# Layer 0's modulation chunks 4 to 11 by ScalarE products and GpSimd sums

## The chip, the cores and the metric

The kernel runs on one core of one Trainium2 chip. The metric is the device time of one execution in microseconds, the median of three runs: 1533.48 before the change (1533.36 to 1533.84). A profile of one execution shows where the time lies. Its engines are PE (TensorE's matmuls), PEld (its weight loads, which overlap PE), DVE (VectorE), ACT (ScalarE), POOL (GpSimd) and SP (SyncE, whose queue starts the loads of weights). Every engine works through its own queue in order.

## The reference

A trunk of two layers works on 512 latent and 256 context tokens of 1024 features. The part that the change touches is the modulation: one vector product for each of two conditions, 6144 columns per layer, which are cut into twelve chunks of 512.

```python
def modulation(cond, w_mod, b_mod):
    m = jax.nn.silu(cond) @ w_mod + b_mod
    return m.reshape(m.shape[:-1] + (N_MOD, D_MODEL))
...
        m_lat = modulation(c, w_mod[l], b_mod[l])
        m_ctx = modulation(c_ctx, w_mod[l], b_mod[l])
        sh1, sc1, ga1, sh2, sc2, ga2 = [m_lat[:, i, None, :] for i in range(N_MOD)]
        csh1, csc1, cga1, csh2, csc2, cga2 = [m_ctx[None, i, None, :] for i in range(N_MOD)]
...
        x_lat = x_lat + ga1 * (jnp.concatenate([attn_lat, gm_lat], axis=-1) @ w_out[l])
        x_lat = x_lat + ga2 * sqrelu_mlp(modulate(rmsnorm(x_lat, norm2_g[l]), sh2, sc2),
                                         w_ff1[l], w_ff2[l])
```

Chunks 0 to 3 are the shift and scale of the first norm. Chunks 4 and 5 are the gate ga1, wanted when the output projection begins. Chunks 6 to 9 are the shift and scale of the second norm, and 10 and 11 the gate ga2 of the MLP. Between norm and gate stand the input projection, a gated mixer (gMLP), grouped-query attention with eight query heads, and one output projection over both. In the last layer the context tokens get no gate and no MLP, so that there only the first four chunks are used for the context condition.

## The kernel before

Activations lie feature by feature, 128 features on the partitions and up to 768 tokens along a row. Every float32 product is made of three passes over numbers split into a high and a low part: `split` casts the high part on ACT (L207) and subtracts it for the low part on DVE or POOL (L208).

The stages of layer 0 follow one another on PE: the first chunks of the modulation and the projection of keys and values, the projections u and g of the mixer, the queries in six banks of 256 tokens, then attention, then the output projection (`proj4`), the second norm, and the MLP with ff1 and ff2. Layer 1 does the same again.

The order of the work around the change is set by `Flow`, an emission clock that counts PE time: `defer` puts work off by so many ns of that clock. Attention is written tile by tile: 16 tiles of context queries (256 keys), then 32 of latent queries (768 keys). A tile is a product of queries and keys (L203, `pa<-B,B`), its maximum on DVE (L825), the exponential on ACT (L828), the reciprocal on DVE (L830), which POOL spreads (`rc`, L833), later transposes on PE (L844) that ACT and DVE split (L846, L847), and then the product with the values (`pb<-A,B`), which closes with a matmul that reads `rc` (L865). After each tile a filler step is emitted on PE. The string `FILL0` orders these fillers: pieces of the output projection of the mixer (`o`, twelve matmuls of 128x384) and pieces of chunks 4 to 11 (`m`).

A piece of `mod_chunk` is one weight block of 128x1024, that is 32x512 matmuls in the four 32-column strips of PE (L326). After four pieces DVE turns the four partial sums (L334), four small matmuls add them (L339), and `mod_store` adds the bias (L391). Its weight blocks use the four slots of the ring `hi`, which the split weights use too.

Layer 1's modulation is made differently: `mod_wide` runs beside the MLP of layer 0. For each half weight block of 128x512 and each condition ACT makes a product with a scalar per partition (L365, L368) into a tile `s`, and POOL adds it to an accumulator (L369). After eight of them DVE turns and sums each condition (L380, L381). The accumulator is one tile in the place `C1`, the raw weights are two halves of a tile `k`. The tiles `s` have three buffers for the whole kernel; the activations of the projections, the mixer and the norms use the same three.

Of the kernel before, what the change touches and what calls it, by code (L numbers as in the profile page):

```python
# [8 lines left out]
F32 = mybir.dt.float32  # L9
# [7 lines left out]
KT = 8  # L17
# [9 lines left out]
# columns of the packed constants  # L27
# [4 lines left out]
# emission lags and periods, in ns of tensor-engine time  # L32
# [9 lines left out]
def once(fn):  # L42
    """fn, but for the first call alone"""
    left = [fn]
    return lambda: left.pop()() if left else None


class Flow:
    """Emission clock: counts tensor-engine time and emits put-off work once its turn has come."""

    def __init__(self):
        self.vt = 0.0
        self.todo = []
        self.n = 0
        self.fillers = []
        self.busy = False

# [5 lines left out]
    def tick(self, ns=0.0):  # L63
# [22 lines left out]
    def fill0(self, until):  # L86
        """pass the time without fillers"""
# [4 lines left out]
    def step(self):  # L92
        """one piece of filler"""
# [9 lines left out]
    def drain(self):  # L103
        """Emit everything put off, with fillers in between."""
# [8 lines left out]
# how pieces of the output projection (o) and of the modulation (m) alternate beside the attention of layer 0  # L113
FILL0 = "oooooooommmommmmmmmmmommmmommmommmomoomo"
# [5 lines left out]
def block_order():  # L120
    o = []
    mod = lambda j: [("mod", 0, j, kb) for kb in range(4)]
    tok = lambda l, g: [("tok", l, g, kb) for kb in range(2)]
    for l in range(DEPTH):
# [10 lines left out]
        if l == 0:  # L135
            o += mod(4) + mod(5)
            rest = mod(6) + mod(7) + mod(8) + mod(9) + mod(10) + mod(11)
            n = 0
            for c in FILL0:
                if c == "m":  # L140
                    o.append(rest.pop(0))
                else:
                    if n % 4 == 0:
                        o.append(("out", 0, 0, n // 4))
                    n += 1
            o += rest
        else:
            o += [("out", l, 0, nb) for nb in range(4)]
        o += [("out", l, 1, nb) for nb in range(4)]
# [11 lines left out]
def trunk(ctx: ExitStack, tc: tile.TileContext, xT, pk1, pk2, rope, wsT, w_mod, w_tok, w_u, w_out, w_ff1, w_ff2, outT):  # L161
# [57 lines left out]
    def convert():  # L219
        """split the oldest block that is held back"""  # L220
# [53 lines left out]
    def rsqrt(v, n):  # L274
        """1/sqrt of a small positive tile: a bit estimate, a quadratic and a cubic step."""
# [26 lines left out]
    # silu of both conditions  # L302
# [12 lines left out]
    def mod_chunk(l, j, lag=1200.0):  # L315
        """512 columns of the modulation of both conditions, four partial sums at a time in the four
        32-column strips of the tensor engine; yields between weight blocks."""
        ps = pb()
        ns = PAR["NS"] if j < 4 else 4
        rows = ns * 32  # L320
        for kb in range(4):
# [6 lines left out]
            if l or j > 3:  # L328
                release()
            if kb < 3:  # L330
                yield
        # 32 by 32 blocks turned, then the strips added
        tr = (tw if l == 0 and j < 4 else tsm)([128, 512])
# [13 lines left out]
    def mod_wide(l):  # L347
        """The modulation of one layer on the vector engine; yields after each half of a weight block."""
        raw = tk([128, 2, 512], F32)

        def load(i):
            j, k = divmod(i, KT)
            if j < 12:
                (nc.gpsimd if PAR["MQ"] else nc.sync).dma_start(raw[:, k % 2, :], w_mod[l, j, k // 2][:, (k % 2) * 512:(k % 2) * 512 + 512])
        load(0)
        for j in range(12):
            acc = unit("C1", [128, 2, 512], F32)
            for k in range(KT):
                w = raw[:, k % 2, :]
# [803 lines left out]
```

## Time and profile before

| | us |
|---|---|
| median of three runs | 1533.48 |
| span of the profiled execution | 1530.9 |
| PE busy in it | 1484.1 |
| DVE busy | 957.4 |
| ACT busy | 682.6 |
| POOL busy | 402.0 |

The span is the time from the first to the last instruction of the profiled execution; 2.6 us lie around it in the median. The matmul rows of PE are pipelined, so that the mean of one is longer than what it adds to the chain. In the chain of work that ended last each step is followed back to what released it. A row of the stretches gives, between two times from the span's start, how long each engine was busy, with the number of instructions in brackets.

### The profile page before, as it was taken

The numbers are of one execution on the slowest core, as the hardware profiler recorded it, in microseconds if no ns is written. First come the engines' busy times: TensorE is split into PE (matmuls) and PEld (weight loads), VectorE is DVE, ScalarE is ACT, GpSimd is POOL, SyncE is SP. The second block draws the span as 40 slices with busy tenths as digits, with TensorE's granted clock in tenths as the row PEclk, the third lists the DMA queues.
The fourth block names the chain that finished last, engine by engine and source line by source line (L and its number), as shares of the span: only waits on it lengthen the run. The fifth ranks groups of instructions, "written<-read, shape, count | busy, mean of one in ns | idle before, by whom it ended". The sixth has DMA issues, their size and how long they took to land.

```text
span 1530.9 us, 22786 instructions
## 1 busy us (share of the span) xinstructions
PE 1484.1 (97%) x8804; PEld 1321.5 (86%) x8804; DVE 957.4 (63%) x1874; ACT 682.6 (45%) x1142; POOL 402.0 (26%) x362
## 2 busy tenths in 40 slices
PE   6999899999999999999999999998999999999998
PEld 2899686779899999999999998996889888888887
DVE  5868966776855555555555547988796644444443
ACT  3542355564545453545444424535784433322221
POOL 0112320023244545545454603035213000000000
PEclk9999999999999999999999999999999999999999
DMA  9221324321134333333333321221101333332332
GB/s 359 67 74 48 119 91 152 110 83 56 62 108 122 113 123 126 111 118 106 124 109 124 98 68 56 86 80 44 41 1 56 97 96 97 98 97 97 96 98 79
DMA packets 49948, 148.83 MB, mean 97 GB/s; under 512 B 5424, under 2 KB 6832, under 8 KB 49840
## 3 DMA queue, kind: packets, MB, share of 16 engines
q1 hardware_dynamic: 49264, 146.46, 29.9%
q8 instruction: 69, 1.13, 0.3%
q10 hardware_dynamic: 576, 0.92, 0.2%
q14 instruction: 39, 0.32, 0.1%
HBM read 145.26 MB, written 2.10 MB: 96 GB/s over the span
## 4 chain that ended last, share of the span: by engine, by line
PE 82%; DVE 12%; DMA 2%; ACT 2%; issue 1%; POOL 0%; SPq 0%; ACTq 0%; POOLq 0%; DVEq 0%
PE pa L203 51%; PE pb L203 21%; PE pt L844 3%; PE pt L203 3%; PE pb L326 2%; DVE lo L208 1%; DMA X<-in_xT 1%; DMA C<-in_w_mod 1%; DVE X L784 1%; DMA A<-in_w_mod 1%; DVE m L277 1%; PE pt L626 1%; DVE B L961 1%; ACT hi L207 1%; PE pb L865 0%
## 5 line engine op out<-in xcount | busy, mean ns | idle before, releaser
L203 PE MATMUL pa<-A,hi 128*128 128x384 f32 (+2 forms) x1696 | 449.2, 347 | 1.7 <-ACT w L954 0.6
L207 ACT CAST hi<-raw 128x1024 fp32r<-128x1024 f32 x171 | 179.5, 1050 | 409.9 <-PE pa L203 326.3
L208 DVE TENSOR_TENSOR lo<-raw,hi 128x1024 fp32r<-128x1024 f32 x155 | 202.7, 1308 | 215.8 <-ACT hi L207 212.4
L203 PEld LDWEIGHTS pa<-A,hi 128*128 128x128 f32 x1696 | 304.7, 188 | 25.9 <-ACT w L954 1.8
L369 POOL TENSOR_TENSOR C<-C,s 128x512 f32<-128x512 f32 x168 | 240.5, 1463 | 245.0 <-ACT s L368 244.8
L203 PE MATMUL pa<-A,lo 128*128 128x384 f32 (+2 forms) x848 | 293.4, 347 | 1.1 <-DVE lo L208 1.1
L203 PE MATMUL pa<-B,hi 128*128 128x384 f32 (+1 forms) x900 | 246.4, 356 | 4.4 <-DVE X L784 4.4
L203 PEld LDWEIGHTS pa<-B,hi 128*128 128x128 f32 x900 | 162.9, 188 | 21.5 <-DVE X L784 9.2
L784 DVE SCALAR_TENSOR_TENSOR X<-pa,modT,X 128x384 f32<-128x384 f32 (+1 forms) x168 | 88.0, 547 | 143.0 <-PE pa L203 143.0
L203 PEld LDWEIGHTS pa<-A,lo 128*128 128x128 f32 x848 | 159.3, 188 | 12.0 <-DVE lo L208 1.3
L203 PE MATMUL pa<-B,lo 128*128 128x384 f32 (+1 forms) x450 | 158.1, 353 | 0.0
L203 PE MATMUL pb<-B,hi 128*128 128x256 f32 (+2 forms) x600 | 152.3, 340 | 0.4 <-DVE X L784 0.4
L368 ACT ACTIVATE s<-k,silu 128x512 f32<-128x512 f32 x168 | 114.3, 716 | 49.4 <-DMA k<-in_w_mod 27.3
L203 PE MATMUL pb<-hi,A 128*128 128x256 f32 x672 | 126.1, 285 | 0.0
L784 DVE SCALAR_TENSOR_TENSOR X<-pb,modT,X 128x512 f32<-128x512 f32 (+3 forms) x116 | 69.1, 602 | 75.8 <-PE pb L203 75.3
L203 PEld LDWEIGHTS pb<-B,hi 128*128 128x128 f32 x600 | 104.0, 189 | 11.6 <-DVE X L784 1.0
L203 PEld LDWEIGHTS pb<-hi,A 128*128 128x128 f32 x672 | 106.1, 191 | 0.2 <-issue 0.2
L203 PE MATMUL pb<-B,lo 128*128 128x256 f32 (+2 forms) x300 | 101.5, 338 | 0.0
L203 PE MATMUL pb<-lo,A 128*128 128x256 f32 x336 | 95.3, 284 | 0.0
L203 PEld LDWEIGHTS pa<-B,lo 128*128 128x128 f32 x450 | 84.4, 188 | 5.8
L847 DVE TENSOR_TENSOR A<-pt,A 128x384 fp32r<-128x384 f32 (+1 forms) x144 | 73.6, 535 | 16.4 <-ACT A L846 14.4
L846 ACT CAST A<-pt 128x384 fp32r<-128x384 f32 (+1 forms) x144 | 64.6, 469 | 43.3 <-PE pt L844 39.5
(169 smaller groups left out, 2300.3 us busy)
## 6 DMA issues: line engine op xcount, KB each, us to landing
raw<-in_w_ff SPq DMA_DIRECT2D x128, 512.0 KB, 3.5
k<-in_w_mod SPq DMA_DIRECT2D x96, 256.0 KB, 3.0
hi<-in_w_mod SPq DMA_DIRECT2D x32, 512.0 KB, 3.6
raw<-in_w_tok SPq DMA_DIRECT2D x19, 512.0 KB, 3.5
raw<-in_w_out SPq DMA_DIRECT2D x16, 512.0 KB, 3.5
A<-in_w_mod SPq DMA_DIRECT2D x8, 512.0 KB, 9.9
raw<-in_w_u SPq DMA_DIRECT2D x8, 512.0 KB, 3.5
B<-in_w_mod SPq DMA_DIRECT2D x6, 512.0 KB, 10.2
```

Source lines behind the costliest of these rows:

```text
L203: pe.matmul(out, a, b, start=start, stop=stop)
L207: act.copy(hi, src)
L208: (eng or vec).tensor_tensor(out=lo, in0=src, in1=hi.bitcast(F32), op=ALU.subtract)
L277: vec.tensor_scalar(yi, v.bitcast(I32), -0.5, 1595932665.0, op0=ALU.mult, op1=ALU.add)
L326: pe.matmul(ps[q:q + 32, :], S32[:, k, :], w[:, k2 * 512:(k2 + 1) * 512], start=k < ns, stop=k >= KT - ns)
L368: act.activation(p, w, AF.Copy, scale=s)
L369: pool_e.tensor_tensor(out=a, in0=a, in1=p, op=ALU.add)
L626: pe.transpose(p[:, o:o + 128], stk[:, t, hh, c0:c0 + 128].bitcast(F32), ident)
L784: vec.scalar_tensor_tensor(out=xs, in0=src[:, s - off:e - off], scalar=modT[l][:, i * 8 + m, cond:cond + 1], in1=xs, op0=ALU.mult, op1=ALU ...
L844: pe.transpose(tp_[:, (kt - k0) * 128:(kt - k0) * 128 + 128], p[:, kt * 128:kt * 128 + 128], ident)
L846: act.copy(pth[:, k0:k0 + step, d], src)
L847: vec.tensor_tensor(out=ptl[:, k0:k0 + step, d], in0=src, in1=pth[:, k0:k0 + step, d].bitcast(F32), op=ALU.subtract)
```

## The change

Chunks 4 to 11 of layer 0 leave PE and are made by `mod_wide`, as layer 1's were. A generator in `Flow.tick` emits one step (half a weight block: two products, two sums) every 4600 ns of the emission clock from the start of layer 0 (`BG`). The turning and summing on DVE is put off by 7000 ns (`MD`), and the small matmuls by another 7000 (`ME`). There are now three raw tiles `mr`, loaded two steps ahead, and two accumulators `macc` in turn. The weight stream has no blocks of chunks 4 to 11 any more. In layer 1 chunks 4 to 11 are made for one condition alone. `FILL0` now says after which tiles a piece of the output projection is emitted. The scratch that dynamic DMA reserves is set to 2048 bytes. Comments and checks of order are left out below.

```diff
+        while self.bg is not None and self.bgt <= self.vt:
+            self.bgt += next(self.bg, 1e9)
...
-FILL0 = "oooooooommmommmmmmmmmommmmommmommmomoomo"
+FILL0 = "1101101101101101" + "01000100010001000100100100100100"
...
-        if l == 0:
-            o += mod(4) + mod(5)
-            rest = mod(6) + mod(7) + mod(8) + mod(9) + mod(10) + mod(11)
...
-        o += [("out", l, 1, nb) for nb in range(4)]
+        o += [("out", l, w, nb) for w in range(2) for nb in range(4)]
...
-        ns = PAR["NS"] if j < 4 else 4
+        ns = PAR["NS"]
...
-    def mod_wide(l):
-        """The modulation of one layer on the vector engine; yields after each half of a weight block."""
-        raw = tk([128, 2, 512], F32)
+    def mod_wide(l, js, period=0.0):
+
+
+        raws = [const.tile([128, 512], F32, tag=f"mr{i}", name=nm("mr")) for i in range(3)] if not mraw else mraw
+        mraw.extend(raws[len(mraw):])
+        steps = [(j, k) for j in js for k in range(KT)]
...
+        for i in range(2):
+            load(i)
+        acc = None
+        for i, (j, k) in enumerate(steps):
+            conds = range(2 if l == 0 or j < 4 else 1)
+            if k == 0:
+                acc = const.tile([128, 2, 512], F32, tag="macc%d" % (j % 2), name=nm("macc"))
+            load(i + 2)
+            w = mraw[i % 3]
+            for cond in conds:
+                a, s = acc[:, cond, :], sc[:, k, cond:cond + 1]
+                if k == 0:
+                    act.activation(a, w, AF.Copy, scale=s)
+                else:
+                    p = tsm([128, 512])
+                    act.activation(p, w, AF.Copy, scale=s)
+                    pool_e.tensor_tensor(out=a, in0=a, in1=p, op=ALU.add)
+            if k < KT - 1:
+                yield period
+                continue
+            fl.defer(PAR["MD"], lambda l=l, j=j, acc=acc, n=len(conds): mod_sums(l, j, acc, n))
+            yield period
+        yield 1e9
+
+    def mod_sums(l, j, acc, n):
+
+        part = tmp.tile([128, 32], F32, tag="mp", name=nm("mp"), bufs=2)[:, 0:16 * n].rearrange("p (c b) -> p c b", c=n)
+        for cond in range(n):
+            tr = tsm([128, 512])
+            vec.transpose(tr, acc[:, cond, :])
+            vec.tensor_reduce(out=part[:, cond, :], in_=tr.rearrange("p (b i) -> p b i", i=32), axis=AX.X, op=ALU.add)
+
+        def fin():
+            p4 = pt((128, n, 4))
...
+        fl.defer(PAR["ME"], fin)
...
-                                fl.step()
+                                if FILL0[nt[0]] == "1":
+                                    fl.step()
+                                nt[0] += 1
                                 fl.fill0(goal)
...
-                fl.fillers = [mods((4, 5)), mixed(fl.fillers[0], mods((6, 7, 8, 9, 10, 11))), fl.fillers[1]]
...
-        wide = None if last else mod_wide(l + 1)
+        wide = None if last else mod_wide(l + 1, range(12))
...
+    fl.bg, fl.bgt = mod_wide(0, range(4, 12), PAR["BG"]), fl.vt
...
-    nc = _bacc.Bacc("TRN2", target_bir_lowering=False, num_devices=1)
+    nc = _bacc.Bacc("TRN2", target_bir_lowering=False, num_devices=1, dynamic_dma_scratch_size=2048)
```

Three places show what this does to the order of the engines. The first is PE's queue where attention begins, before the change: `pa<-B,B` are the first tiles' products of queries and keys, `32x512` the pieces of chunk 4, `pt<-c,w` the transposes of the first tiles.

```order
L203 MATMUL pa_2082<-B_107_486,B_249_1611 128x256
L203 MATMUL pa_2082<-B_108_487,B_249_1611 128x256
L326 MATMUL pb_2094<-hi_1853,S_86 32x512 x2
L626 MATMUL pt_2097<-c_70,k_2035 128x128 x4
L626 MATMUL pt_2103<-c_70,k_2035 128x128 x4
L203 MATMUL pa_2116<-B_107_486,B_249_1611 128x256
L203 MATMUL pa_2116<-B_108_487,B_249_1611 128x256
L326 MATMUL pb_2094<-hi_1855,S_86 32x512 x2
L326 MATMUL pb_2094<-hi_2130,S_86 32x512 x2
L326 MATMUL pb_2094<-hi_2132,S_86 32x512 x2
L844 MATMUL pt_2111<-c_70,w_2087 128x128 x2
```

The same place now, where `128x384` is the first piece of the output projection, `A` the mixer's split output and `mp` the sums of chunk 6.

```order
L193 MATMUL pa_2305<-B_107_486,B_295_1766 128x256
L193 MATMUL pa_2305<-B_108_487,B_295_1766 128x256
L193 MATMUL pb_2329<-A_388_2317,hi_2038 128x384
L381 MATMUL pt_2343<-mp_2176,c_70 32x8 x4
L627 MATMUL pt_2349<-c_70,k_2251 128x128 x4
L193 MATMUL pa_2380<-B_107_486,B_295_1766 128x256
L193 MATMUL pb_2329<-A_388_2317,hi_2038 128x384
L193 MATMUL pb_2329<-A_388_2317,lo_2039 128x384
L193 MATMUL pb_2329<-A_389_2320,hi_2038 128x384
L193 MATMUL pa_2380<-B_108_487,B_295_1766 128x256
```

The pieces of the modulation are gone, and the output projection of the mixer stands in their place, ahead of the first transposes. Over the whole kernel PE's queue has 39 rows fewer.

The second place is POOL's queue at the first context tiles, before the change. `rc` spreads a reciprocal, `lo` is the low part of a weight block of the output projection, `k` that of a query bank.

```order
L833 COPY rc_2092<-m_2090 128x64
L833 COPY rc_2126<-m_2124 128x64
L833 COPY rc_2092<-m_2151 128x64
L833 COPY rc_2126<-m_2176 128x64
L208 TENSOR_TENSOR lo_2242<-raw_2239,hi_2241 128x1024
L833 COPY rc_2215<-m_2213 128x64
L208 TENSOR_TENSOR lo_2275<-raw_2272,hi_2274 128x1024
L833 COPY rc_2255<-m_2253 128x64
```

The same place now; `macc` is an accumulator, `s` a product from ACT.

```order
L835 COPY rc_2315<-m_2313 128x64
L615 TENSOR_TENSOR k_2407<-w_2187,k_2407 128x8x64
L362 TENSOR_TENSOR macc_2148<-macc_2148,s_2416 128x512
L835 COPY rc_2390<-m_2388 128x64
L362 TENSOR_TENSOR macc_2148<-macc_2148,s_2419 128x512
L835 COPY rc_2315<-m_2430 128x64
L362 TENSOR_TENSOR macc_2148<-macc_2148,s_2495 128x512
L835 COPY rc_2390<-m_2448 128x64
L362 TENSOR_TENSOR macc_2148<-macc_2148,s_2498 128x512
L835 COPY rc_2511<-m_2509 128x64
L362 TENSOR_TENSOR macc_2148<-macc_2148,s_2549 128x512
```

A sum of the modulation now stands between each two `rc`. POOL has 24 such sums between the first and the last `rc` of the context tiles and 28 among those of the latent tiles. Ahead of the first `rc` it has 46, and the low parts of the first four weight blocks of the output projection now stand there too, of which it had none there before. ACT's queue has 54 products ahead of the first exponential, 26 among the 16 context tiles, 34 among the 32 latent tiles and 14 from there to the start of the MLP.

The third place is DVE's queue in the fourth of the six query banks, before the change (`m` are sums and roots of a row, `G` the rotation's table).

```order
L593 TENSOR_REDUCE m_1888<-s_1886 128x8
L597 TENSOR_TENSOR w_1890<-pb_1816,G_150 128x512
L601 TENSOR_TENSOR s_1892<-pb_1816,G_150 128x8x32 x2
L606 TENSOR_SCALAR m_1888<-m_1888 128x8
L602 TENSOR_TENSOR w_1890<-w_1890,s_1892 128x512
L277 TENSOR_SCALAR m_1897<-m_1888 128x8
L280 TENSOR_TENSOR m_1899<-m_1897 128x8
L281 SCALAR_TENSOR_TENSOR m_1899<-m_1899,m_1888 128x8
```

The same bank now.

```order
L594 TENSOR_REDUCE m_2086<-s_2084 128x8
L598 TENSOR_TENSOR w_2088<-pb_1992,G_150 128x512
L602 TENSOR_TENSOR s_2090<-pb_1992,G_150 128x8x32 x2
L607 TENSOR_SCALAR m_2086<-m_2086 128x8
L375 STREAM_TRANSPOSE s_2177<-macc_1536 128x512
L603 TENSOR_TENSOR w_2088<-w_2088,s_2090 128x512
L267 TENSOR_SCALAR m_2095<-m_2086 128x8
L376 TENSOR_REDUCE mp_2176<-s_2177 128x16
L270 TENSOR_TENSOR m_2097<-m_2095 128x8
L375 STREAM_TRANSPOSE s_2180<-macc_1536 128x512
L271 SCALAR_TENSOR_TENSOR m_2097<-m_2097,m_2086 128x8
L376 TENSOR_REDUCE mp_2176<-s_2180 128x16
```

The two transposes and two sums of chunk 6 now lie inside this bank's work. Those of chunks 4 and 5 lie earlier, in the mixer's projections, and those of 7 to 11 later.

More of the change, by code (lines that the diff above doesn't have):

```diff
@@ L457, in apply @@
             l, w, off, n, cond = self.l, self.w, self.off, self.n, self.cond
+            assert all((l, w * 6 + k // 4 + i) in stored for k in ks for i in (0, 2))
             B = lambda k: modT[l][:, w * 24 + k, cond:cond + 1]
@@ L898, in gm_out @@
             yield from proj4(("out", l, 0), GM, 2, [dense], "b")
-        def mods(js):
-            for j in js:
-                yield from mod_chunk(0, j)
-        def mixed(a, b):
-            for c in FILL0:
-                next(a if c == "o" else b)
-                yield
-            yield from a
-            yield from b
         if last:
```

67 lines of the change are left out of this document (16 added, 51 removed), and 2 rows, old and new, of the table PAR.

## The prediction

> **What bounds the kernel now.** First the page's busy times and its chain, to see which engine sets the end.
>
> ```profile
> span 1530.9 us, 22786 instructions
> PE 1484.1 (97%) x8804; PEld 1321.5 (86%) x8804; DVE 957.4 (63%) x1874; ACT 682.6 (45%) x1142; POOL 402.0 (26%) x362
> PE 82%; DVE 12%; DMA 2%; ACT 2%; issue 1%; POOL 0%; SPq 0%; ACTq 0%; POOLq 0%; DVEq 0%
> ```
>
> PE is busy for 97% of the span, so work taken from PE counts unless something takes its place. Next the table of stretches, cut where the stages of layer 0 change: mixer's projections to 121 us, queries to 178, context tiles to 226, latent tiles, their tail with the output projection, second norm, start of the MLP, the MLP. The last row is a stretch of layer 1's attention.
>
> ```profile
> core 0: us, PE busy (x) PEld busy (x) DVE busy (x) ACT busy (x) POOL busy (x), PEclk, DMA share, GB/s
> 56.00:121.00 65.00, 64.34 (x463) 62.30 (x462) 50.60 (x166) 31.83 (x59) 8.87 (x8) 1.00 0.22 66
> 121.00:178.00 57.00, 56.61 (x471) 55.26 (x470) 49.22 (x158) 19.52 (x31) 16.04 (x12) 1.00 0.16 47
> 178.00:226.00 48.00, 40.60 (x258) 32.33 (x257) 32.87 (x92) 24.60 (x68) 14.07 (x22) 0.93 0.40 134
> 226.00:338.00 112.00, 110.43 (x694) 78.30 (x693) 79.07 (x168) 64.73 (x143) 16.52 (x35) 1.00 0.36 118
> 338.00:376.00 38.00, 37.97 (x259) 34.15 (x258) 22.61 (x51) 16.26 (x33) 12.02 (x13) 1.00 0.13 42
> 376.00:402.00 26.00, 25.02 (x153) 21.82 (x151) 20.36 (x42) 11.66 (x22) 7.72 (x5) 1.00 0.19 62
> 402.00:440.00 38.00, 36.97 (x181) 32.38 (x182) 27.95 (x43) 22.28 (x35) 7.81 (x5) 1.00 0.28 87
> 440.00:900.00 460.00, 456.49 (x2677) 447.80 (x2676) 247.88 (x337) 216.19 (x289) 232.64 (x164) 1.00 0.37 114
> 1100.00:1140.00 40.00, 39.84 (x295) 36.41 (x293) 37.92 (x81) 36.19 (x83) 6.92 (x22) 1.00 0.00 1
> ```
>
> PE bounds all of layer 0 but 178 to 226, where it idles 7.4 us. DVE is close behind it in the query banks (49.2 of 57). ACT and POOL have room everywhere. The last row shows that this kernel can run PE at 99.6% with DVE at 95% and ACT at 90%.
>
> **What PE loses.** The group of L326 over the layer's `hi` blocks, and two rows of the chain, one a piece of the modulation and one a piece of the output projection:
>
> ```profile
> L326 PE MATMUL pb<-hi,S 128*32 128x512 f32 x128 | 36.6, 612 | 0.9 <-DMA hi<-in_w_mod 0.9
> 288.48 0.98 PE pb L326 x4
> 236.20 2.09 PE pb L203 x12
> ```
>
> 128 matmuls are 32 pieces of four. The 36.6 us count pipelined overlap; a piece stands 0.98 us in the chain, so 32 x 0.98 = **31.4 us** leave PE. The small adding matmuls stay, four to a chunk. In the new order 8 of the pieces leave the context tiles and 24 the latent ones.
>
> **What ACT, POOL and DVE gain.** The new kind of work is the one that layer 1's modulation does during the MLP:
>
> ```profile
> 479.24 1.94 ACT L368 ACTIVATE s<-k,silu 128x512 f32<-128x512 f32 x3
> L369 POOL TENSOR_TENSOR C<-C,s x164: 1272/1294/2328, 439.0 to 876.1; 128x512 f32<-128x512 f32 x164
> L369 POOL TENSOR_TENSOR C<-C,s 128x512 f32<-128x512 f32 x164 | 233.7, 1456 | 204.8 <-ACT s L368 204.7
> L380 DVE STREAM_TRANSPOSE s<-C 128x512 f32<-128x512 f32 x24 | 16.8, 701 | 0.0
> L381 DVE TENSOR_REDUCE m<-s 128x16 f32<-128x512 f32 x24 | 16.4, 685 | 0.8
> ```
>
> A product costs ACT 1.94 / 3 = 0.65 us, a sum costs POOL 1.29 alone and 2.33 at worst, 1.46 on average, and a chunk's two conditions cost DVE 2 x (0.70 + 0.69) = 2.8 us. Now stage by stage.
>
> *To 178 us.* ACT gets 54 products, 35 us, into 122 us of which 51 are used: hidden. POOL gets 46 sums, 67 us, and four low parts of 2.39 (below), beside 25 us: hidden too. DVE isn't: chunks 5 and 6 put 5.6 us into the stretch from 121 to 178. Beside that, sums on POOL and subtractions on DVE slow one another. The rows of the MLP's second low part, beside POOL, and of the query banks:
>
> ```profile
> L961 DVE TENSOR_TENSOR B<-w,B x22: 957/1930/1940, 480.4 to 891.3; 128x768 fp32r<-128x768 f32 x22
> L608 DVE TENSOR_TENSOR w<-w,m 128x512 f32<-128x512 f32 x5 | 5.0, 994 | 0.2
> L602 DVE TENSOR_TENSOR w<-w,s 128x512 f32<-128x512 f32 x4 | 2.7, 686 | 0.0
> L208 DVE TENSOR_TENSOR lo<-raw,hi 128x1024 fp32r<-128x1024 f32 x2 | 2.4, 1220 | 0.0
> ```
>
> L961 takes 0.96 us at its shortest and 1.93 at its median, so one meeting costs up to 0.97. The stretch has 5 + 4 + 2 = 11 such operations with two operands outside PSUM: 0 to 10.7 us, and with POOL busy for about half of the time I take 5. DVE then needs 49.2 + 5.6 + 5 = 60 of 57. Its 7.8 idle us are mostly waits that stay. I take **+6**, with bounds 0 (its idle time takes all) and +16 (none of it). [...]
>
> *178 to 226.* PE loses 8 x 0.98 and, by a count in the order, has 132 matmuls of 128x384 among the context tiles where it had 96, three pieces of twelve more: 40.6 - 7.8 + 3 x 2.09 = 39. ACT: 24.6 + 26 x 0.65 = 41.5. POOL:
>
> ```profile
> 195.34 2.39 POOL L208 TENSOR_TENSOR lo<-raw,hi 128x1024 fp32r<-128x1024 f32 x1 [1.51 <-ACT hi L207]
> 337.87 0.24 POOL L833 COPY rc<-m 128x64 f32<-128x64 f32 x1 [2.62 <-DVE m L830]
> 186.64 0.69 PE L844 MATMUL pt<-c,w 128*128 128x128 f32 x2 [4.75 <-ACT w L828]
> ```
>
> POOL had 14.1 us here; 24 sums at 1.46 make 35, and two more low parts fall into the stretch, 4.8: 54 us, more than the 48. An `rc` takes 0.24 us, but it now waits behind sums, and PE's closing matmul of a tile pair (L865) waits for `rc`, with every later tile queued behind it; ACT's next products wait for POOL too, by the three `s` tiles, with exponentials behind them. So POOL ends last: 54 for 48, **+6**. With all sums at 1.29 and PE's floor it is -2, with all at 2.33 (75 us) it is +27. The 4.75 us before the first transposes was ACT waiting behind DVE's split of the mixer output; that split stays, so I leave the wait in.
>
> *226 to 338.* PE loses 24 x 0.98 = 23.5 and two pieces of 2.09, and gains four context pieces of the output projection that come forward from the tail:
>
> ```profile
> 353.53 5.75 PE pb L203 x48
> ```
>
> Those are four pieces, 5.75 us. PE: 110.4 - 23.5 - 4.2 + 5.8 = 88.5. ACT: 64.7 + 34 x 0.65 - 3 = 84, three casts of weights having moved up. DVE stays at 79 to 84: six transposes of 0.7 go, two chunks' sums of 2.8 come, and the rest is what POOL may hold up. POOL 16.5 + 28 x 1.46 - 5 = 52. Three engines within 5 us of each other could run like the last row of the table, but the 34 products are spread unevenly, with some ten tiles free of them, so ACT leads in one part and PE in the other. I take 94 for 112: **-18**. Bounds: -23.5 (PE's floor) and 0.
>
> *338 to 402.* The four pieces are gone from the tail, -5.8. They covered the last tiles' exponential, split and values; I give 2 back for that. The second norm sums its squares on POOL, and eight of the modulation's sums now lie between these:
>
> ```profile
> 371.00:393.00 22.00, 21.59 (x113) 18.14 (x112) 17.97 (x36) 10.36 (x18) 10.02 (x6) 1.00 0.21 72
> ```
>
> 10.0 + 8 x 1.29 = 20.3 of 22 us: full, so the norm ends about 2 late. Together **-2**, bounds -6 and +6.
>
> *The MLP, 402 to 900.* 64 products and 64 sums fewer, and two accumulators.
>
> ```profile
> PE pa L203 <- DVE X L784: 4.4, 5, 1.2
> L365 ACT ACTIVATE C<-k,silu 128x512 f32<-128x512 f32 x22 | 14.6, 713 | 53.4 <-DVE s L380 53.4
> ```
>
> ACT's 53.4 us of waiting for the one accumulator go, but PE idles only 3.5 us from 440 to 900 and waited 4.4 from 402 on for DVE's gates. **-2**, bounds -4 and 0. The loads carry the same bytes in smaller pieces on a queue that is under half full (DMA share 0.16 to 0.40): nothing, as long as ACT frees the raw tiles in time; if not, the cost is in the terms above.
>
> Sum: 6 + 6 - 18 - 2 - 2 = -10. The profiled execution would go from 1530.9 to 1521, and with the 2.6 us around it (1533.5 - 1530.9) the median to **1523**.
>
> **Rivals.**
> 1. *The cover holds, PE sets everything.* DVE's idle time takes the sums and POOL keeps up: 0 - 2 - 23.5 + 0 - 2 = -27.5, so 1506; with all lower bounds -35.5, 1498. For it: the 99.6% of the layer 1 row. Against: DVE's 86% in the query banks and POOL's 54 us.
> 2. *It cancels.* ACT's products and PE's fillers don't interleave in the latent tiles, which then take 105: 6 + 6 - 7 - 2 - 2 = +1, so 1534.
> 3. *Slower: POOL's queue paces the context tiles.* The sums take 2.33 as beside L961, POOL needs 75 us for 48, and `rc` holds PE: +27 with the rest as forecast (6 - 18 - 2 - 2 = -16) is +11, so 1544. It decides from a mean sum of about (48 + 16 - 19) / 24 = 1.9 us. Against: in the attention few DVE operations have two operands outside PSUM. PE's clock fell with the 4.75 us wait, to 0.93 over 178 to 226, which is 3.4 us lost; longer waits for `rc` would repeat that. [...]
>
> That the change doesn't do what it says is excluded by the order, in which L326 has only the first four chunks left.
>
> **How the numbers follow.** Forecast 0.52 (1514 to 1529), rival 1 0.17, rival 2 0.13, rival 3 0.18. About 0.2% (3 us) is what a measurement of this kernel can tell from no change. So faster 0.69, same 0.13, slower 0.18. The range of 1502 to 1545 takes in rival 1 but for its far end, rival 2, and the nearer half of rival 3; about 0.13 is left out.
>
> **What would show it.** Right: DVE's last query bank ends some 6 us later; POOL is nearly full in the context tiles, whose last exponential comes about 12 us later than now counted from the start; the latent tiles take 94 us from first to last product of queries and keys; PE's idle time moves to `rc`. Wrong: PE idle under the 4.75 us at the start of attention, sums on POOL at 1.3 us, or latent tiles at 110 us with ACT as releaser.

## The result, and the profile after

The changed kernel takes **1576.1 us** (median of 4 runs, 1574.5 to 1577.9) beside 1533.4 us (4 runs, 1532.4 to 1533.8) before: a ratio of 1.028, interval 1.026 to 1.029. I had forecast 1523 in a range of 1502 to 1545; the change makes the kernel slower by 43 us. The page of the changed kernel, its first part, the clock by slice, and the chain of work that ended last:

```profile
span 1572.7 us, 22711 instructions
...
PE 1470.2 (93%) x8676; PEld 1332.0 (85%) x8676; DVE 1001.7 (64%) x1882; ACT 717.0 (46%) x1206; POOL 469.3 (30%) x418
...
PEclk9899879999999999999999999999999999999999
...
PE 69%; DVE 17%; ACT 6%; POOL 2%; issue 2%; DMA 2%; SPq 0%; ACTq 0%; POOLq 0%; DVEq 0%
```

PE's busy time fell by 14 us where 31 were taken off it, mostly because the clock is down in slices 5 and 6 (157 to 236 us; a matmul of 128x256 takes 0.41 us at a granted clock of 0.50 and 0.28 at 1.00); DVE's share of the chain rose from 12% to 17%. To see where the 41.8 us of span came from I cut the execution at the exponentials of layer 0's attention. Their line, in the kernel before and in the changed one (count; shortest, median and longest in ns; start of the first and of the last in us):

```profile
L828 ACT ACTIVATE w<-pa,m x48: 473/902/919, 186.0 to 348.8; 128x768 f32<-128x768 f32 x32, 128x256 f32<-128x256 f32 x16
```

```profile
L830 ACT ACTIVATE w<-pa,m x48: 456/902/962, 235.8 to 385.3; 128x768 f32<-128x768 f32 x32, 128x256 f32<-128x256 f32 x16
```

The attention starts 49.8 us later, runs 13.3 us shorter (149.5 for 162.8), and what is behind it takes 5.3 us longer (1187.4 for 1182.1). So the loss lies ahead of the attention, where the matmuls are nearly the same in both kernels: before, 16 of chunk 4 stand there, and now 19 of the output projection and 24 small adding ones. The same stretches as a table, first of before (56 us to the first exponential), then of the changed kernel:

```profile
56.00:186.00 130.00, 123.92 (x950) 118.57 (x948) 107.61 (x338) 52.94 (x93) 29.27 (x22) 1.00 0.23 74
```

```profile
56.00:235.80 179.80, 139.39 (x980) 133.30 (x979) 151.09 (x354) 89.73 (x149) 95.61 (x71) 0.90 0.25 80
56.00:121.00 65.00, 55.95 (x388) 53.03 (x387) 52.16 (x130) 39.84 (x71) 30.39 (x25) 0.97 0.26 82
121.00:160.00 39.00, 33.26 (x240) 32.27 (x239) 26.93 (x83) 19.42 (x30) 20.02 (x16) 0.91 0.27 89
160.00:236.00 76.00, 50.38 (x357) 48.20 (x356) 72.17 (x144) 30.67 (x48) 45.19 (x31) 0.82 0.22 73
236.00:386.00 150.00, 133.99 (x900) 120.82 (x899) 120.25 (x266) 124.67 (x278) 90.25 (x108) 0.95 0.23 70
```

Read the columns as time, then PE, PEld, DVE, ACT, POOL, then the granted clock, the DMA share and GB/s. DVE has 43.5 us more to do (151.1 for 107.6) and fills 72 of the 76 us from 160 to 236. PE idles 40.4 us where it idled 6.1, and it is busy for 15.5 us longer (139.4 for 123.9) at a clock of 0.90; the matmuls that both kernels have there account for 13.1 of these (134.0 for 120.9). What PE waited for between 56 us and the first exponential, by line (us in total, times, longest):

```profile
PE pb L193 <- DVE A L776: 9.4, 1, 9.4
PE pt L627 <- POOL k L615: 7.4, 3, 3.3
PE pb L193 <- DVE s L602: 4.8, 2, 4.2
PE pb L193 <- ACT A L775: 4.6, 1, 4.6
```

DVE's 43.5 us: the sums over partitions are 8.3 of them (6 transposes and 6 reductions). Most of the rest sits where I hadn't looked, in `rsqrt` (L267 to L277, nine operations on tiles of 4 or 8 columns a time). One of its lines from 56 us to the first exponential, before and after:

```profile
L280 DVE TENSOR_TENSOR m<-m x15: 144/164/168, 64.3 to 184.7; 128x4 f32<-128x4 f32 x9, 128x8 f32<-128x8 f32 x6
```

```profile
L270 DVE TENSOR_TENSOR m<-m x15: 151/165/2271, 64.9 to 233.0; 128x4 f32<-128x4 f32 x9, 128x8 f32<-128x8 f32 x6
```

The median stays at 0.165 us, and the longest goes from 0.168 to 2.27. Over all lines of `rsqrt`, from the start to the first exponential, 151 operations take 63.1 us where they took 28.4, and 33 of them are over 0.9 us where 3 were. The timeline shows what happens in such a one (start, us, engine, line, operation):

```profile
196.61 1.15 DVE L267 TENSOR_SCALAR m<-m 128x8 int32<-128x8 int32 x1
...
197.70 2.35 POOL L198 TENSOR_TENSOR lo<-raw,hi 128x1024 fp32r<-128x1024 f32 x1
197.80 2.27 DVE L270 TENSOR_TENSOR m<-m 128x8 f32<-128x8 f32 x1
...
200.01 1.26 POOL L615 TENSOR_TENSOR k<-w,k 128x512 fp32r<-128x512 f32 x1
200.10 1.18 DVE L271 SCALAR_TENSOR_TENSOR m<-m,m 128x8 f32<-128x8 f32 x1
...
201.23 2.52 POOL L362 TENSOR_TENSOR macc<-macc,s 128x512 f32<-128x512 f32 x2
...
201.32 1.10 PE L627 MATMUL pt<-c,k 128*128 128x128 f32 x8 [3.08 <-POOL k L615]
201.32 1.19 DVE L272 SCALAR_TENSOR_TENSOR m<-m,m 128x8 f32<-128x8 f32 x1
```

Each of these small operations begins shortly after POOL has begun one of its own and ends just after it (17 to 31 ns for all of `rsqrt` that were held up so): 197.80 + 2.27 = 200.07 against 197.70 + 2.35 = 200.05. The next POOL operation starts (200.01) before the next one of DVE (200.10), which waits again.

PE's longest wait stands right behind such a chain. A matmul of the output projection, which the new order puts ahead of the attention, needs the mixer's split output `A`, and VectorE makes that behind the `rsqrt` of a query bank:

```profile
216.84 1.23 DVE L267 TENSOR_SCALAR m<-m 128x8 int32<-128x8 int32 x1
...
224.66 2.26 DVE L277 SCALAR_TENSOR_TENSOR m<-m,m 128x8 f32<-128x8 f32 x1
...
226.96 2.79 DVE L609 TENSOR_TENSOR w<-w,m 128x512 f32<-128x512 f32 x1
229.67 1.81 DVE L776 TENSOR_TENSOR A<-C,A 128x768 fp32r<-128x768 f32 x2
...
230.67 0.69 PE L193 MATMUL pb<-A,hi 128*128 128x384 f32 x1 [9.44 <-DVE A L776]
```

This `rsqrt` takes 10.1 us from its first operation to the end of its last; with nothing beside it in the trace of before one takes 1.8.

### The profile page after: what moved, and what is told of

It is laid out like the page before. It is cut to its first block, busy times and chain, and to the rows that moved or that the text cites. A ratio compares the mean times of both kernels' runs of the same rounds, so it can differ in the third digit from the quotient of the medians.

```text
span 1572.7 us, 22711 instructions
## 1 busy us (share of the span) xinstructions
PE 1470.2 (93%) x8676; PEld 1332.0 (85%) x8676; DVE 1001.7 (64%) x1882; ACT 717.0 (46%) x1206; POOL 469.3 (30%) x418
## 4 chain that ended last, share of the span: by engine, by line
PE 69%; DVE 17%; ACT 6%; POOL 2%; issue 2%; DMA 2%; SPq 0%; ACTq 0%; POOLq 0%; DVEq 0%
PE pa L193 49%; PE pb L193 15%; PE pt L846 2%; PE pt L193 2%; ACT s L361 1%; DVE lo L198 1%; POOL macc L362 1%; ACT w L830 1%; ACT hi L197 1%; ACT A L848 1%; DVE m L270 1%; DVE m L267 1%; DVE B L955 1%; DVE X L786 1%; DMA raw<-in_w_tok 1%
## 5 line engine op out<-in xcount | busy, mean ns | idle before, releaser
L362 POOL TENSOR_TENSOR macc<-macc,s 128x512 f32<-128x512 f32 x224 | 313.4, 1415 | 359.0 <-ACT s L361 356.2
L198 DVE TENSOR_TENSOR lo<-raw,hi 128x1024 fp32r<-128x1024 f32 x155 | 196.1, 1265 | 220.2 <-ACT hi L197 216.9
L193 PEld LDWEIGHTS pa<-B,hi 128*128 128x128 f32 x900 | 162.8, 188 | 25.9 <-DVE X L786 13.6
L361 ACT ACTIVATE s<-mr,silu 128x512 f32<-128x512 f32 x224 | 154.6, 719 | 61.2 <-DVE mp L376 21.0
L193 PE MATMUL pb<-hi,A 128*128 128x256 f32 x672 | 130.6, 290 | 6.8 <-DVE s L602 4.8
L193 PE MATMUL pb<-A,hi 128*128 128x512 f32 (+2 forms) x288 | 86.8, 381 | 14.6 <-DVE A L776 9.4
L428 POOL TENSOR_TENSOR acc<-acc,s 128x256 f32<-128x256 f32 (+1 forms) x43 | 45.2, 1052 | 157.9 <-ACT s L426 157.3
```

The costliest lines, as they stand in the source:

```text
L193: pe.matmul(out, a, b, start=start, stop=stop)
L198: (eng or vec).tensor_tensor(out=lo, in0=src, in1=hi.bitcast(F32), op=ALU.subtract)
L361: act.activation(p, w, AF.Copy, scale=s)
L362: pool_e.tensor_tensor(out=a, in0=a, in1=p, op=ALU.add)
L428: eng.tensor_tensor(out=self.acc, in0=self.acc, in1=sq, op=ALU.add)
```

## Experiments

**Theory 1**: GpSimd's additions hold up VectorE's small operations; VectorE becomes the bound of the query banks; TensorE idles and its clock falls. **Theory 2**: ScalarE's products hold the three shared `s` buffers until their addition is done. **Theory 3**: GpSimd's own later work (`k`, `B`, `C`) is late behind additions. **Theory 4**: the sums over partitions on VectorE.

All numbers in a table; its text follows. `rsqrt` is the busy time of its lines up to the first exponential. The runs that leave something out or exchange it were taken once each, beside times of before of 1531.5 (the e1 runs) to 1533.6.

| run | first exponential | last | rsqrt us | span | time us |
|---|---|---|---|---|---|
| before | 186.0 | 348.8 | 28.4 | 1530.9 | 1533.4 |
| changed | 235.8 | 385.3 | 63.1 | 1572.7 | 1576.1 |
| e1_noadd | 198.6 | 336.3 | 36.5 | 1516.5 | 1518.3 |
| e1_memset | 203.1 | 343.2 | 41.1 | 1524.8 | 1526.6 |
| e4_memset3 | 212.9 | 352.7 | 52.1 | 1536.9 | 1538.7 |
| e1_addraw | 239.2 | 387.7 | 67.2 | 1572.6 | 1574.4 |
| e4_halves | 234.9 | 385.7 | 57.9 | 1575.1 | 1577.1 |
| e1_short | 210.4 | 362.6 | 9.6 | 1541.0 | 1542.8 |
| e2_before_short | 180.2 | 345.7 | 3.9 | 1516.2 | 1518.0 |
| e5_recip | 214.5 | 365.8 | 37.0 | 1548.5 | 1550.3 |
| e5_nosums | 232.7 | 367.0 | 62.4 | 1556.5 | 1558.3 |

### The additions left out, or replaced

```diff
 # e1_noadd
-                    pool_e.tensor_tensor(out=a, in0=a, in1=p, op=ALU.add)
+                    if l:
+                        pool_e.tensor_tensor(out=a, in0=a, in1=p, op=ALU.add)
 # e1_memset: and for layer 0
+                    else:
+                        pool_e.memset(a, 0.0)
 # e1_addraw
-                    pool_e.tensor_tensor(out=a, in0=a, in1=p, op=ALU.add)
+                    pool_e.tensor_tensor(out=a, in0=a, in1=p if l else w, op=ALU.add)
```

e1_noadd: 

> The changed kernel, but GpSimd's additions of chunks 4 to 11 of layer 0 are left out (224 - 112 stay, those of layer 1), so these chunks of the modulation hold their first product alone; ScalarE's products, the loads and the sums over partitions stay. Theory 1 (GpSimd's additions hold up VectorE's small operations on tiles outside PSUM): the rsqrt operations fall from 60.5 us back to about 26, the first exponential goes from 235.8 back to 188 to 198 (the chunk sums, 8.3 us, and ScalarE's products stay), and the time to 1525 to 1540. Theory 2 (ScalarE, whose in-order products wait for the three shared buffers that an addition holds) and theory 3 (GpSimd's queue makes its own later work late) expect the same here; theory 4 (the chunk sums on VectorE) and ScalarE's products as the price expect no recovery, 1565 to 1576.

e1_memset: 

> The changed kernel, but each of the 112 GpSimd additions of layer 0 is replaced by GpSimd writing zeros to the accumulator: chunks 4 to 11 of layer 0 are zero but for the order. GpSimd's queue keeps its entries and their place, reads no tile, and the product's buffer comes free when ScalarE has written it. Theory 1 expects the rsqrt operations near 26 to 32 us, a first exponential before 200 and 1525 to 1540, if it is the reading that excludes VectorE; 1560 or more if writing does too. Theory 3 (the length of GpSimd's queue) expects a recovery only in proportion to the time that the writes are shorter than the 1.4 us of an addition.

e1_addraw: 

> The changed kernel, but layer 0's GpSimd additions add the raw weight tile, not ScalarE's product: the sums of chunks 4 to 11 of layer 0 leave the factors out. Same number, shape and time of additions, but none of them holds one of the three buffers that the products share with other work, and none waits for ScalarE. Theory 1 expects no recovery: rsqrt operations at 55 us or more, first exponential at 225 to 240, 1565 to 1580. Theory 2 (the shared buffers and ScalarE's order) expects a first exponential before 205 and 1530 to 1545.

Without the additions the time is 1518.3, better than theory 1 had it, and the attention starts at 198.6, just past its range (`rsqrt` stays over its 26 us, beside the POOL work that is left); products, loads and sums over partitions are all still there, so 37.2 of the 49.8 us hang on the additions (235.8 - 198.6). The new order of PE's queue is there as well, and the two waits for `A`, 9.4 and 4.6 us in the changed kernel, shrink to 2.5 and 1.4 in total; so the order alone isn't the price. Theory 4 in its full form falls. With the raw tile added, no `s` buffer is held and no addition waits for a product, and nothing recovers: theory 2 falls. With zeros written, most recovers (203.1, where theory 1 had less than 200, and `rsqrt` at 41.1). But a write took 0.53 us where an addition takes 1.4, so the queue of POOL was shorter too, which leaves theory 3. Three writes for each addition make it as long:

```diff
 # e4_memset3, for layer 0
-                        pool_e.memset(a, 0.0)
+                        for _ in range(3):
+                            pool_e.memset(a, 0.0)
```

> The changed kernel, but each of layer 0's 112 GpSimd additions is replaced by three writes of zeros to the accumulator (0.53 us each in e1_memset, 1.6 us in all against 1.4 to 1.5 of an addition): the queue of GpSimd is as long as in the changed kernel, but reads no tile for these chunks, which come out as zeros but for the order. Theory 1 (the additions' reads hold up VectorE): rsqrt operations at 36 to 46 us before the first exponential, which comes at 198 to 212, and 1518 to 1538. Theory 3 (GpSimd's own later work comes late): as the changed kernel, first exponential at 225 to 240 and 1560 to 1580.

212.9 and 1538.7 lie just past the edge of what theory 1 expected (`rsqrt`, at 52.1, well past its 46), far from theory 3; yet it is 14 us later than with no additions at all. The lines of the `rsqrt` give one reason. The line of its second TENSOR_SCALAR, and the timeline around the longest:

```profile
L275 DVE TENSOR_SCALAR m<-m x15: 159/210/6578, 65.6 to 212.7; 128x4 f32<-128x4 f32 x9, 128x8 f32<-128x8 f32 x6
```

```profile
186.76 8.24 POOL L366 MEMSET macc<- 128x512 f32 x17
...
186.88 0.17 DVE L273 TENSOR_TENSOR m<-m 128x8 f32<-128x8 f32 x1
187.08 0.17 DVE L274 TENSOR_TENSOR m<-m,m 128x8 f32<-128x8 f32 x1
187.28 6.58 DVE L275 TENSOR_SCALAR m<-m 128x8 f32<-128x8 f32 x1
```

Beside the writes from 180 to 188 us the two-operand operations of `rsqrt` keep their 0.12 to 0.17 us; its TENSOR_SCALARs are lengthened, one to 0.39 us (L267), and one stood for 6.58 us: it begins 0.52 us into the row of 17 writes and ends at 193.86, 1.14 us before the row does. So this run doesn't free VectorE wholly. Theory 3 isn't removed: the 14.3 us beyond e1_noadd are a mixture of its share and of the 15.6 us by which `rsqrt` grew (52.1 - 36.5).

### The small operations shortened, or exchanged

```diff
 # e1_short (changed kernel) and e2_before_short (kernel before), in rsqrt
-        t, r = small(n), small(n)
-        vec.tensor_tensor(out=t, in0=y, in1=y, op=ALU.mult)
...
-        vec.scalar_tensor_tensor(out=y, in0=t, scalar=1.875, in1=y, op0=ALU.add, op1=ALU.mult)
 # e5_recip: in place of these eight
+        t = small(n)
+        for _ in range(4):
+            vec.reciprocal(t, y)
+            vec.reciprocal(y, t)
```

e1_short: 

> The changed kernel, but each reciprocal square root is its bit estimate alone: the eight operations of its two refinement steps are left out, so norms are off by a few per cent. Some 120 of 135 small VectorE operations go, 54 us of the 60.5 in the changed kernel (23 of the 25.5 in the kernel before, where they would be worth a third of that). Theory 1: VectorE is the engine that paces 160 to 236 us and most of its small operations go, so the first exponential falls by 25 to 45 us to 190 to 210, and the time to 1530 to 1550. Theories 2 and 3 (ScalarE's buffers, GpSimd's queue): by 10 us at most, 1564 or more.

e2_before_short: 

> The kernel before, with each reciprocal square root as its bit estimate alone (the two refinement steps left out, so norms are off by a few per cent), the control of e1_short. There the cut was worth 33 us. Theory 1 (GpSimd's additions lengthen these operations, 28.4 us of them before the first exponential in the kernel before against 63.1 in the changed one): here it is worth 4 to 15 us, 1518 to 1528, the first exponential at 174 to 183. If the refinement steps cost the same whatever GpSimd does, 25 to 35 us, 1498 to 1508, and e1_short says nothing of the additions.

e5_recip: 

> The changed kernel, but the eight operations of the two refinement steps of each reciprocal square root are replaced by eight reciprocals in turn (y, 1/y, y, ...), so the result is the bit estimate as in e1_short, and VectorE has as many operations as in the changed kernel. In its trace reciprocals of one column kept their length beside GpSimd (164 ns against 156), as did all operations that read PSUM or reduce. Theory 1 (small operations of the held-up forms wait out GpSimd's operation): the rsqrt operations fall from 63 us to 25 to 35, the first exponential comes at 208 to 222, time 1540 to 1556. If the number of operations is the price (and e1_short's gain came from having fewer), or if reciprocals of 4 and 8 columns are held up too: 230 or later, 1568 to 1580.

The cut brings the attention forward by 25.4 us in the changed kernel and by 5.8 in the kernel before. That is the interaction theory 1 asks for, though both also gain 8 to 10 us later. The third run is the sharpest: as many VectorE operations as in the changed kernel, the same additions on POOL, only another form, and the first exponential is at 214.5. The reciprocals stand beside POOL at their full speed (five of 0.18 us from 158.72 to 159.75, during an addition from 158.55 to 159.82):

```profile
L271 DVE RECIPROCAL m<-m x136: 134/178/205, 20.2 to 1201.3; 128x4 f32<-128x4 f32 x76, 128x8 f32<-128x8 f32 x40, 128x2 f32<-128x2 f32 x20
```

So for these operations form decides, not number. It gives back 21.3 us of the 49.8 (235.8 - 214.5). The rest of what hangs on the additions, 15.9 us (214.5 - 198.6), stays, although `rsqrt` is down to 37.0, as in e1_noadd (36.5). TensorE's wait for `k`, which GpSimd makes, is the largest difference; e5_recip first, then e1_noadd:

```profile
PE pt L622 <- POOL k L610: 7.5, 3, 4.0
```

```profile
PE pt L628 <- POOL k L616: 0.6, 1, 0.6
```

That is theory 3's mechanism. It likely makes up much of the 15.9 us; no run separates it.

In the changed kernel's trace to 240 us, beside a POOL operation that had begun first, two-operand operations outside PSUM (L270 to L274, L276, L277, L603, L609) and TENSOR_SCALARs (L267, L275, L607) were held up until it ended: those of `rsqrt` took up to 2.27 us there and 0.12 to 0.17 with nothing beside them, L603 up to 1.48 for 0.42, L609 up to 2.85 for 0.69, L607 up to 1.02 for 0.16. Those with an operand in PSUM kept their length (L598 0.68 us, L602 0.41 to 0.42, and on 512 columns L677 0.68 to 0.69, L681 0.65 to 0.69), as did reductions (L376 0.67), transposes (L322, L375: 0.70 to 0.71) and reciprocals (of one column there, 0.16). Why one form is held up and another isn't, no run shows.

### Shorter additions, and the sums left out

```diff
 # e4_halves, for layer 0
-                    pool_e.tensor_tensor(out=a, in0=a, in1=p, op=ALU.add)
+                    for h in ((0, 256), (256, 512)) if l == 0 else ((0, 512),):
+                        pool_e.tensor_tensor(out=a[:, h[0]:h[1]], in0=a[:, h[0]:h[1]], in1=p[:, h[0]:h[1]], op=ALU.add)
 # e5_nosums
+            if l == 0:
+                act.copy(part[:, cond, :], acc[:, cond, 0:16])
+                continue
             tr = tsm([128, 512])
             vec.transpose(tr, acc[:, cond, :])
```

e4_halves: 

> The changed kernel, but each of layer 0's additions is split in two of 256 columns: 224 shorter operations with the same elements. If VectorE waits for the end of the operation that GpSimd is in, a small operation waits half as long: rsqrt operations fall from 63 us to 40 to 50, the first exponential to 210 to 228, the time to 1550 to 1568. [...]

e5_nosums: 

> The changed kernel, but the transposes and reductions of layer 0's chunks 4 to 11 are left out; ScalarE copies 16 columns of the accumulator in their place, so these chunks of the modulation hold one column of 32 of the sums. 12 VectorE operations, 8.3 us, go before the first exponential. Theory 4 in its full form (the sums are the price) expects a first exponential near 190 and 1530; theory 1 expects about these 8.3 us, 225 to 231 and 1563 to 1570.

Halves don't help: 1.0285 times before, interval 1.0268 to 1.0301, as slow as whole additions. Counting the `rsqrt` operations that begin while an addition runs: 26 of mean 1112 ns in the changed kernel, 52 of mean 577 with halves. Over their free 160 ns that is 26 x 0.952 = 24.8 us against 52 x 0.417 = 21.7. Each wait halves, as theory 1 says, but twice as many operations run into one. I had left out that a chain of nine can meet a POOL operation at step after step, as the one from 196.61 us above does at its first five.

The sums cost 3.1 us ahead of the attention, but 15.2 us in it (149.5 to 134.3 from first to last exponential): a miss on both counts. VectorE's waits in the attention of the changed kernel name the place:

```profile
DVE m L832 <- ACT w L830: 9.8, 19, 1.6
DVE s L375 <- POOL macc L362: 6.3, 5, 1.9
```

A transpose that waits for the last addition heads VectorE's queue: 6.3 us of waiting, beside some 10 us of transposes and reductions. The clock is in it too: 0.95 over the attention of the changed kernel, and 1.00 there without the sums and without the additions alike, so that the prices of the two overlap and don't add up.

### Layer 1 alone, and fewer chunks

```diff
 # e3_layer1: layer 0 as before, layer 1 as changed. e3_wide8, e3_wide6: chunks from 8 or from 6, from the attention on
-    fl.bg, fl.bgt = mod_wide(0, range(4, 12), PAR["BG"]), fl.vt
...
+                fl.fillers = [mods((4, 5)), mixed(fl.fillers[0], mods(PEJ)), fl.fillers[1]]
+                fl.bg, fl.bgt = mod_wide(0, range(8, 12), PAR["BG"]), fl.vt
 # e4_layer1_one: e3_layer1, and
-                acc = const.tile([128, 2, 512], F32, tag="macc%d" % (j % 2), name=nm("macc"))
+                acc = const.tile([128, 2, 512], F32, tag="macc0", name=nm("macc"))
...
-            fl.defer(PAR["MD"], lambda l=l, j=j, acc=acc, n=len(conds): mod_sums(l, j, acc, n))
+            mod_sums(l, j, acc, len(conds))
 # e4_wide8b: e3_wide8, layer 1 by the function of before, and
-"BG": 6000.0
+"BG": 4600.0
```

e3_layer1: 

> Layer 0 as in the kernel before (chunks 4 to 11 on TensorE beside the attention); only layer 1's modulation has the changed code: three own raw tiles, two accumulators in turn, one condition for chunks 4 to 11, sums over partitions put off. My prediction's last term: 2 us gained, 1528 to 1534, first exponential at 186. The rival reads the 5 us that the changed kernel lost behind its attention as the price of this code (eight GpSimd additions in a row, four VectorE operations of the sums in a block): 1535 to 1540.

e4_layer1_one: 

> e3_layer1 with one accumulator in place of two, and the sums over partitions issued right behind the last product of a chunk. Theory 1 for layer 1: with two accumulators GpSimd runs a chunk's additions in one row and holds VectorE's products r*r and their differences (956 to 1135 and 1536 to 1840 ns) for longer; with one, the next chunk's additions wait for the transposes, these operations fall back towards 956 and 1536, and the time to 1532 to 1535. If the four operations of the sums in a block are the price, it stays at 1536 to 1538.

e3_layer1 is 1.0018 times before, interval 1.0009 to 1.0027: some 2.8 us slower, though a third of layer 1's additions is gone. TensorE's waits in the MLP (440 to 900 us) for the gates, before and in e3_layer1:

```profile
PE pa L203 <- DVE X L784: 3.4, 4, 1.2
```

```profile
PE pa L208 <- DVE X L803: 7.2, 5, 1.5
```

The product r*r (L960 before) never took over 0.959 us; here:

```profile
L984 DVE TENSOR_TENSOR w<-w x25: 949/958/1881, 477.6 to 893.6; 128x768 f32<-128x768 f32 x25
```

With one accumulator and the sums issued at once, its longest is 0.961 us and the ratio 1.0004 (0.9994 to 1.0014). The waits only fell to 6.0, and the two intervals overlap. So the direction is likely, and the split between the accumulators and the time of issue isn't shown.

e3_wide8: 

> Chunks 4 to 7 of layer 0 on TensorE beside the attention as before; only chunks 8 to 11 by ScalarE products and GpSimd sums, which start with the attention, one step of 2 products every 6 us; layer 1 as in the changed kernel. Nothing of them stands beside the query banks. Theory 1: the first exponential is back at 186 to 188; the attention loses 16 TensorE pieces (15.7 us), and pays for the additions. In the changed kernel 44 additions lay in the attention, which took 11.8 us longer than with the additions left out, 0.27 us each; 56 of them cost 15 us at that price, less where VectorE has room: 1520 to 1532. A first exponential later than 195 or a time over 1540 speaks against theory 1.

e3_wide6: 

> As e3_wide8, but chunks 6 to 11 by ScalarE and GpSimd from the attention's start, one step every 4.6 us; chunks 4 and 5 on TensorE. 24 TensorE pieces (23.5 us) go, 84 additions come: at 0.27 us each 23 us, at half of it 11. Theory 1: first exponential at 186 to 188 and 1518 to 1532, at or under e3_wide8 if the additions cost less beside the attention than 0.27 us.

e4_wide8b: 

> e3_wide8 with layer 1's modulation as in the kernel before, and a step of layer 0's chunks 8 to 11 every 4.6 us in place of 6, so that chunks 8 and 9 are complete before the norm that reads them. e3_wide8 was 1531.2, of which e3_layer1 puts 3.3 on layer 1's code: 1526 to 1530, first exponential at 186. If the earlier finish of chunks 8 and 9 also takes idle time of TensorE behind the attention away, 1523 to 1527.

In these three runs the order of the fillers changed with the chunks, and e4_wide8b has one buffer `mp` where the changed kernel has two. With nothing of the new work ahead of the attention, the first exponential is at 186.1, 188.0 and 188.2. e3_wide8 is 0.9987 times before (0.9977 to 0.9996). e3_wide6 misses its range: 1547.2 us, 1.0091 (1.0074 to 1.0107). Its attention is 7.8 us shorter than before (155.0 for 162.8), but behind it the work lasts 1202.7 us for 1182.1. The 110 us behind its last exponentials, and behind those of e4_wide8b:

```profile
343.00:453.00 110.00, 97.30 (x532) 84.94 (x531) 80.19 (x135) 63.23 (x106) 58.99 (x45) 0.92 0.27 85
```

```profile
340.50:450.50 110.00, 106.20 (x617) 95.33 (x617) 76.37 (x139) 51.54 (x86) 37.49 (x28) 1.00 0.23 73
```

In e3_wide6 products and additions still run beside the second norm and the start of the MLP (ACT 63, POOL 59 us), TensorE idles 12.7 us and its clock is 0.92; its longest wait there, 4.3 us, is for ScalarE (`w`, L979). **e4_wide8b beats both kernels**: 1526.2 us (1524.9 to 1528.3), 0.9955 times before, interval 0.9942 to 0.9968.

## Why the prediction was wrong

1. *"32 x 0.98 = 31.4 us leave PE"*: they did, and the attention kept less than half of it. For 178 to 338 I had +6 - 18 = -12, and first to last exponential became 13.3 us shorter. That the totals are so close is luck. First to last exponential of the context tiles went from 39.0 to 41.6 us, so +2.6 for my +6, and the latent tiles' products of queries and keys from 118.7 to 104.7, so -14.0 for my -18 (their stage ran past my cut at 338). My +6 was POOL's queue holding `rc`, and no matmul waited for `rc` (in its rows ACT alone did, 0.3 us). The price lay in the additions (without them the attention takes 137.7 us, 11.8 fewer) and in the sums (15.2 fewer without).
2. The term *"To 178 us"*, +6 with bounds 0 and +16, is **the step that failed**: the first exponential came 49.8 us later. I wrote that the stretch has "5 + 4 + 2 = 11 such operations with two operands outside PSUM". I had picked the long ones from the costliest groups. An operation that waited lost the rest of POOL's operation (0.95 us in the mean of the 26 of `rsqrt` that began beside an addition, 0.16 us long when free), so the count decides: beside the 11 there were 72 operations of `rsqrt` in that stretch (121 to 178 us), 151 up to the first exponential. Their growth, 34.7 us, is the larger part of DVE's 43.5. The trace of before had it in small: three operations of `rsqrt` over 0.9 us, where the others take 0.16. The 11 that I counted grew by 2.7 us in all, less than my 5, nearly all of it in one line, of before and then of the changed kernel:

```profile
L608 DVE TENSOR_TENSOR w<-w,m x5: 691/692/2204, 151.8 to 176.5; 128x512 f32<-128x512 f32 x5
```

```profile
L609 DVE TENSOR_TENSOR w<-w,m x5: 691/691/2848, 182.7 to 227.0; 128x512 f32<-128x512 f32 x5
```

I had misread the first of these rows as well: its mean of 994 ns hid one of 2.20 us, a meeting that cost 1.5 us and not "up to 0.97".

3. The second part of the same step: I let DVE's excess pass to PE one for one, and ended there. The clock was in rival 3 alone, for the context tiles. PE's waits of 9.4, 4.6 and 4.2 us came while VectorE was at the query banks; the clock went to 0.82 there (160 to 236 us), and PE was busy for 15.5 us more. By these three waits the granted clock is 0.50, from 186.0 to 192.8 and from 216.7 to 233.8 us, but the length of a gap alone doesn't decide: behind one of 2.0 us, which ends at 417.4, the granted clock is 0.50 from 418.1 to 421.5 us, and behind one of 3.1, which ends at 201.3, it stays at 1.00 until 216.7. No run here separates the clock from the idle time before it.
4. Rival 3, the one on the slower side, had the right engine and the wrong place and victim: POOL's additions took 1.30 us on average in the attention, under its 1.9 and my 1.46, and the context tiles weren't where the time went. My lower bound there, -2, doesn't follow either: with all sums at 1.29 POOL needs 14.1 + 4.8 + 31.0 = 49.9 of 48 us. e1_noadd, e1_addraw and e5_recip show the hold-up of VectorE ahead of them instead.
5. The term of the MLP, -2 with bounds -4 and 0: the sign was wrong, +2.8 in e3_layer1. I had credited ACT's 53.4 us of waiting for the accumulator, which nothing waited for, and missed that those waits likely kept POOL's additions apart. Nor are 64 sums gone, but 56: the first product of a chunk goes straight into the accumulator.
6. What stays open: of the 37.2 us that hang on the additions, 21.3 are shown to go through `rsqrt` (e5_recip); the other 15.9, with GpSimd's late `k` among them, weren't taken apart. Of the 12.6 us by which e1_noadd still starts its attention late, e5_nosums puts 3.1 on the sums; the rest (products on ACT, loads, the new order, the clock at 0.96) wasn't taken apart either.

## What to carry to other kernels

Before moving work to GpSimd, count every VectorE operation that it will stand beside with two operands in SBUF (or a TENSOR_SCALAR between SBUF tiles), the shortest ones first. Here the 26 of `rsqrt` that began beside an addition lost 0.95 us each in the mean, and in the chain of nine from 216.84 us, shown above in part, six operations took 1.2 to 2.3 us in place of 0.17. Look too at what GpSimd itself has to deliver behind the new work. In this kernel the additions were cheaper beside the attention, where operations that read PSUM make 94 of VectorE's 120 us: 52 of them cost 11.8 us there, and the 46 ahead of it 37.2, where such operations make 37 of 151. VectorE's own work can take a form that isn't held up where there is one, as the reciprocals here (0.13 to 0.21 us). An idle time that looks like waste may be what keeps two engines apart; for layer 1's accumulator that is likely, not shown.

## What the runs showed of the hardware that I had not expected

- A held-up operation didn't always get its turn after one GpSimd operation: in e4_memset3 a TENSOR_SCALAR of 128x8 took 6.58 us in a row of 17 writes of 0.53 us. Two-operand ones kept 0.17 us there.
- In e5_recip reciprocals of 128x2, 128x4 and 128x8 took 0.13 to 0.21 us in all 136 uses of their line, beside GpSimd or not.
- Splitting GpSimd's additions in two changed the hold-up little (24.8 to 21.7 us), since twice as many operations met one (26 and 52).
